# A streaming-encoder layer on one core: rows normalised before the up projection, its convolution read from PSUM, the embedding product placed in front of it

## Chip, cores and metric

The kernel runs on one core of a Trainium2 chip. The metric is the device time of one execution in microseconds (us); several executions are made and their median is given. The profile is of one execution.

## The reference, cut to what matters

The input is 2048 rows of 1024 columns in float32. One layer is computed:

```
x = x + concat(conv mixer, RWKV-7 mixer)(rms_norm(x) @ w_in) @ w_out
u = causal_dwconv(rms_norm(x) * ffn_norm_g @ ffn_w_up, conv_w) + conv_b      # width 3 in time, 5632 columns
x = x + (silu(u[:, :2816]) * u[:, 2816:]) @ ffn_w_down
e = rms_norm(p @ ple_w_proj)                                                # p has 256 columns
x = x + sigmoid(rms_norm(x) @ ple_w_gate) * e
out = rms_norm(x)
```

rms_norm divides each row of x by the root of the mean of its squares and multiplies by a gain per column. The convolution takes, for each column, the value of this time step and of the two before it.

## The kernel before

Everything lies transposed: columns of x on the 128 partitions, time along the free dimension. Time is cut into four groups (g) of G = 512 steps. A product is made in three matmuls for each 128x128 block of the weight (`mm3`, lines 187 to 193), since weight and row are each split into a high and a low part of type fp32r: hi x hi, hi x lo, lo x hi. An up product has 8 blocks, 24 matmuls of 128x512, and lands in one PSUM tile of tag "d" in the pool `psd` (3 buffers, line 940), which it shares with the down products (`ps_d`), the embedding's products (`ps_e`) and the sums of the norms (`ps_norm`).

Weights are loaded in halves of 128x1024 (`half`, lines 156 to 173), 4 buffers, each for 12 matmuls. In group 0 a half is loaded from the input, its high part is a ScalarE cast and its low part a GpSimd subtraction (line 154), and the pair is stored to DRAM; in groups 1 to 3 the pair is loaded by a DMA that GpSimd issues (line 161).

A dense group is `dense_rest` (line 387), a generator:

- output projection: 8 products over the rows of y; VectorE adds x from DRAM (line 395) to give tile x2[m]. `rows.add` (line 404) then squares it (ScalarE, line 227), adds the squares up (VectorE, line 229) and splits x2[m] times its gain into hi (ScalarE, line 214) and lo (VectorE, line 215). These rows are not yet divided by the root mean square.
- up projection: 44 products in 22 pairs (`act_pair`, line 423; gate column block i and value block 22 + i), whose result is multiplied by rstd behind the product. rstd (lines 233 to 251) is a matmul of the summed squares with a matrix of ones, then a chain of ScalarE Ln, Exp and Square, each of the first two with a table load, and three VectorE operations. The first two up products don't wait for it: `product` (lines 269 to 288) copies them to SBUF (`raw`, line 281) and issues the norm behind the second (HELD = 2).
- the evacuation of an up product (lines 409 to 420): VectorE multiplies PSUM by rstd into `zb` (line 255), a tile with two more columns in front; GpSimd copies the last two columns of the previous group there (line 256) and keeps this group's last two (line 257); ScalarE multiplies by the third tap and adds the bias (line 412); VectorE adds the two other taps by shifted reads of `zb` (line 417, twice). A pair then goes through tanh (line 429), two VectorE products (lines 430 and 433) and a split into hi and lo (lines 153 and 154).
- down projection (`down`, line 440) in six stages: after every second pair of a block of four, 8 products of 12 matmuls over the four pairs before; VectorE adds them to x2 (line 457).
- embedding: `ple_rows` (line 348) loads two tiles of p and splits them after the second pair; `ple_embed` (line 358) makes 8 products of 6 matmuls after the third pair, in four weight quads with a yield after each; ScalarE copies each to SBUF (line 370), stores it to DRAM (line 371) and squares it. Its rstd comes after the fourth pair.
- gate projection: 8 products, then the last norm and the store of the output, which is issued within the next group (line 405).

Beside it runs the RWKV mixer as a second generator, `rwkv_unit`, in 16 units of 128 time steps: some 41 steps each, small matmuls with long chains of VectorE, ScalarE and DMA between them. `drive` (line 978) lets it take one step for each yield of the dense generator (0.85 in the output and gate projections). It ends shortly before group 3's dense work.

TensorE's instructions stay in program order (`pin`, line 91). The order on the other engines, and the slots of the pools, are set at build time by a scheduler that takes, by a model of time, what is ready and first in priority; most evacuations and norms are marked as high priority. The pool of 128x512 work tiles (`buf`, line 198) has 6 buffers, that of the split rows (`slot`, line 206) 32.

## Time and profile before

| | us |
|---|---|
| median of 3 runs | 2909.51 (2909.09 to 2910.27) |
| the profiled execution | 2908.45 |
| its span in the trace | 2906.5 |
| TensorE busy | 2768.1 (95%) |
| VectorE busy | 1908.3 (66%) |
| GpSimd busy | 1117.4 (38%) |
| ScalarE busy | 959.9 (33%) |

The span runs from the first instruction to the last; the rest of the execution lies around it. PE is TensorE's matmuls, PEld its weight loads, DVE VectorE, ACT ScalarE, POOL GpSimd, SP the engine that issues most loads. The input projection fills the first 700 us; the four dense groups begin at 700.7, 1297.8, 1865.2 and 2419.2 us. A matmul's recorded duration contains its way through the array, so neighbours overlap, and a busy TensorE in the table is not one at its peak.

### The profile page before, as it was taken

What the parts mean: (1) busy time and instruction counts of PE and PEld (TensorE: products, weight loads), DVE (VectorE), ACT (ScalarE), POOL (GpSimd) and SP (SyncE); (2) the same over time, 40 slices, a digit from 0 to 9 for tenths busy, and PEclk for the clock granted to TensorE, in tenths of its full rate; (3) what the DMA queues carried; (4) which work ended last, traced back from release to release, by engine and by line L of the source; (5) the groups of instructions that cost most, each with busy time, mean ns of one, the idle gap of its engine ahead of it and who ended that gap; (6) DMA issues with size and microseconds to landing.
All of it is one profiled execution on the core that took longest, in us unless ns stands there. A gap on an engine that the chain in (4) does not pass through costs nothing.

```text
span 2906.5 us, 42153 instructions
## 1 busy us (share of the span) xinstructions
PE 2768.1 (95%) x15464; PEld 2226.7 (77%) x15464; DVE 1908.3 (66%) x3039; ACT 959.9 (33%) x1721; POOL 1117.4 (38%) x1700
## 2 busy tenths in 40 slices
PE   8999999999889999989999999999999999999997
PEld 5778888778677877767778887777788877788885
DVE  5575665648587868796766676857676765544446
ACT  5332232312553433443412223434222143411113
POOL 4533232324556565652333333333333332433221
PEclk9999999999999999989999999999999999999998
DMA  8887777767777777767666565766565668666665
GB/s 298 297 261 217 236 214 223 209 210 243 263 252 245 258 241 247 248 228 230 178 186 185 173 192 172 233 202 200 174 192 169 187 187 266 216 195 189 196 188 169
DMA packets 285802, 629.95 MB, mean 217 GB/s; under 512 B 60186, under 2 KB 113690, under 8 KB 285596
## 3 DMA queue, kind: packets, MB, share of 16 engines
q0 software_dynamic: 95040, 346.07, 39.4%
q1 hardware_dynamic: 134144, 232.83, 24.0%
q10 hardware_dynamic: 56412, 48.36, 5.2%
q8 instruction: 122, 2.00, 0.3%
q14 instruction: 84, 0.69, 0.1%
HBM read 467.77 MB, written 159.38 MB: 216 GB/s over the span
## 4 chain that ended last, share of the span: by engine, by line
PE 50%; DVE 22%; DMA 14%; issue 6%; ACT 5%; POOL 3%; ACTq 1%; SPq 0%; DVEq 0%; POOLq 0%
PE ps_mm L86 33%; PE ps_d L86 11%; DVE uf L417 3%; DVE pd L794 3%; DVE xs L798 2%; DMA lm<-ld 1%; DMA xd<-xs 1%; DMA ld<-ltt 1%; DVE zb L255 1%; DVE sq L229 1%; DMA es<-e 1%; PE o_ps L86 1%; DMA dt<-xd 1%; DVE lo L215 1%; DMA x<-in_xT 1%
## 5 line engine op out<-in xcount | busy, mean ns | idle before, releaser
L86 PE MATMUL ps_mm<-hi,whlu 128*128 128x512 f32 x2816 | 910.6, 397 | 11.3 <-POOL whlu L154 5.1
L86 PEld LDWEIGHTS ps_mm<-hi,whlu 128*128 128x128 f32 x2816 | 532.3, 189 | 131.9 <-POOL whlu L154 7.8
L86 PE MATMUL ps_mm<-hi,whlin 128*128 128x512 f32 x1664 | 542.9, 400 | 19.6 <-ACT whlin L153 7.1
L86 PE MATMUL ps_mm<-lo,whlu 128*128 128x512 f32 x1408 | 552.3, 392 | 1.5 <-DVE lo L215 1.5
L86 PE MATMUL ps_d<-hi,whld 128*128 128x512 f32 x1408 | 456.1, 396 | 16.7 <-DMA whld<-kd 7.2
L86 PEld LDWEIGHTS ps_mm<-hi,whlin 128*128 128x128 f32 x1664 | 316.7, 190 | 93.0 <-ACT whlin L153 7.1
L417 DVE SCALAR_TENSOR_TENSOR uf<-zb,vec,uf 128x512 f32<-128x512 f32 x352 | 298.6, 851 | 89.6 <-ACT uf L412 78.4
L86 PE MATMUL ps_mm<-lo,whlin 128*128 128x512 f32 x832 | 328.9, 395 | 2.8 <-DVE lo L215 2.8
L412 ACT ACTIVATE uf<-zb,vec 128x512 f32<-128x512 f32 x176 | 143.1, 815 | 562.0 <-DVE zb L255 536.8
L86 PEld LDWEIGHTS ps_d<-hi,whld 128*128 128x128 f32 x1408 | 265.6, 189 | 79.2 <-DVE x L457 8.4
L86 PEld LDWEIGHTS ps_mm<-lo,whlu 128*128 128x128 f32 x1408 | 266.8, 189 | 56.2 <-DVE lo L215 2.4
L161 POOL DMA_DIRECT2D whlu<-ku x264 | 141.7, 537 | 436.8 <-PE ps_mm L86 289.1
L255 DVE TENSOR_TENSOR zb<-ps_mm,rstd 128x512 f32<-128x512 f32 x216 | 148.5, 688 | 208.0 <-PE ps_mm L86 204.4
L86 PE MATMUL ps_d<-lo,whld 128*128 128x512 f32 x704 | 275.4, 391 | 0.0
L457 DVE TENSOR_TENSOR x<-ps_d,x 128x512 f32<-128x512 f32 x192 | 131.6, 687 | 139.5 <-PE ps_d L86 138.7
L86 PEld LDWEIGHTS ps_mm<-lo,whlin 128*128 128x128 f32 x832 | 158.4, 190 | 38.1 <-DVE lo L215 6.6
L161 POOL DMA_DIRECT2D whlin<-kin x156 | 84.1, 539 | 248.9 <-PE ps_mm L86 207.7
L86 PE MATMUL ps_mm<-hi,whlg 128*128 128x512 f32 x512 | 169.2, 406 | 3.4 <-DMA whlg<-kg 3.4
L86 PE MATMUL ps_mm<-hi,whlo 128*128 128x512 f32 x512 | 163.1, 397 | 8.5 <-DMA whlo<-ko 4.9
L154 POOL TENSOR_TENSOR lo<-th,hi 128x512 fp32r<-128x512 f32 x88 | 115.2, 1310 | 110.9 <-ACT hi L153 110.3
L154 POOL TENSOR_TENSOR whlu<-rawu,whlu 128x512 fp32r<-128x512 f32 x88 | 122.6, 1398 | 88.9 <-ACT whlu L153 79.2
L86 PEld LDWEIGHTS ps_d<-lo,whld 128*128 128x128 f32 x704 | 133.2, 189 | 26.0
(205 smaller groups left out, 4248.0 us busy)
## 6 DMA issues: line engine op xcount, KB each, us to landing
whlu<-ku POOLq DMA_DIRECT2D x264, 512.0 KB, 4.5
whlin<-kin POOLq DMA_DIRECT2D x156, 512.0 KB, 4.8
whld<-kd POOLq DMA_DIRECT2D x132, 512.0 KB, 4.0
ku<-whlu SPq DMA_DIRECT2D x88, 512.0 KB, 4.7
kin<-whlin SPq DMA_DIRECT2D x52, 512.0 KB, 5.3
whlo<-ko POOLq DMA_DIRECT2D x48, 512.0 KB, 5.5
whlg<-kg POOLq DMA_DIRECT2D x48, 512.0 KB, 3.9
rawu<-in_w_up SPq DMA_DIRECT2D x88, 256.0 KB, 4.1
```

Of the source, the lines that this page charges most:

```text
L86: return pin(nc.tensor.matmul(*args, **kw))
L154: nc.gpsimd.tensor_tensor(out=lo, in0=raw, in1=hi.bitcast(F32), op=ALU.subtract)
L161: nc.gpsimd.dma_start(out=t, in_=kept[key])
L215: nc.vector.scalar_tensor_tensor(out=lo, in0=src, scalar=gcol, in1=hi.bitcast(F32), op0=ALU.mult, op1=ALU.subtract)
L229: nc.vector.tensor_tensor(out=sq, in0=sq, in1=self.acc, op=ALU.add)
L255: nc.vector.tensor_tensor(out=zb[:, 2 : G + 2], in0=ps, in1=rstd, op=ALU.mult)
L412: nc.scalar.activation(u, zb[:, 2 : G + 2], AF.Identity, bias=v("ffn_conv_b", n), scale=v("ffn_conv_w", 88 + n),)
L417: nc.vector.scalar_tensor_tensor(out=u, in0=zb[:, d : d + G], scalar=v("ffn_conv_w", 44 * d + n), in1=u, op0=ALU.mult, op1=ALU.add,)
L457: nc.vector.tensor_tensor(out=x2[m], in0=ps, in1=x2[m], op=ALU.add)
L794: tt(out=pd[:, :, :, 0:n], in0=xs[:, :, None, 0:n].broadcast_to([P, 8, 2, n]), in1=lm[:, None, i : i + 2, 0:n].broadcast_to([P, 8, 2, n]), ...
L798: nc.vector.tensor_reduce(out=xs[:, :, i : i + 2], in_=pd[:, :, :, 0:n], op=ALU.add, axis=mybir.AxisListType.X,)
```

## The change

- The output stage only sums the squares; it no longer splits rows. After the fifth output product (m = 4) the p tiles are loaded and split.
- After the output products come the first quad of the embedding, a yield, the norm's matmul and chain, and then, for each of the 8 rows, a VectorE product x2 * gain * rstd, a ScalarE cast to hi and a subtraction to lo, on VectorE for even and GpSimd for odd rows. The three other quads of the embedding follow, and only then the up products. The embedding's own norm comes after the first pair.
- An up product is evacuated from PSUM without zb: ScalarE makes tap and bias, and copies the last two columns to u_last; VectorE adds two columns from the new tile `halo` to the first two and then adds the two other taps with the PSUM tile itself as shifted input. `halo` is made for all 44 products at once, in four operations of 128x44, in front of the rows.

```
--- before.py
+++ after.py
@@ -18,7 +18,7 @@
 G = 512
 KD = 8
 FIN = 1
-PLE_AT = 2
+PLE_ROWS = 4
 HELD = 2
 WAIT = 20
 R_BONUS = 1
@@ -142,6 +142,7 @@
     z_last = cpool.tile([P, 14], F32, tag="z_last", name="z_last")
     cx_last = cpool.tile([P, 4, 2], F32, tag="cx_last", name="cx_last")
     u_last = cpool.tile([P, 44, 2], F32, tag="u_last", name="u_last")
+    halo = cpool.tile([P, 44, 2], F32, tag="halo", name="halo")
     for t in (z_last, cx_last, u_last):
         nc.vector.memset(t, 0.0)
 
@@ -388,7 +389,7 @@
         tmp = pools["tmp"]
         gs = slice(g * G, (g + 1) * G)
         x2 = []
-        rows = Rows()
+        rows, ss = Rows(), SumSq()
 
         def evac_o(ps, _):
             t = pools["x2"].tile([P, G], F32, tag="x2", name=f"x2_{g}_{len(x2)}")
@@ -401,22 +402,55 @@
                 xs.append(staged(pools, xT[m, :, gs], "xr"))
             for _ in product(pools, weight(pools, w_out[m], f"o{m}"), yrows, evac_o):
                 yield SLOW
-            rows.add(pools, x2[m], v("ffn_norm_g", m))
+            ss.add(pools, x2[m])
             if m == FIN and pending:
                 pending.pop()()
+            if m == PLE_ROWS:
+                prows = ple_rows(pools, g)
+
+        embedding = ple_embed(pools, g, prows)
+        next(embedding)
+        yield
+        rstd = ss.rstd(pools)
+        with tc.high_priority():
+            w0, w1 = v("ffn_conv_w", 0, 44), v("ffn_conv_w", 44, 44)
+            nc.vector.tensor_tensor(out=halo[:, :, 1], in0=u_last[:, :, 1], in1=w0, op=ALU.mult)
+            nc.vector.tensor_tensor(out=halo[:, :, 0], in0=u_last[:, :, 1], in1=w1, op=ALU.mult)
+            nc.vector.tensor_tensor(out=u_last[:, :, 0], in0=u_last[:, :, 0], in1=w0, op=ALU.mult)
+            nc.vector.tensor_tensor(
+                out=halo[:, :, 0], in0=halo[:, :, 0], in1=u_last[:, :, 0], op=ALU.add
+            )
+            for k in range(KD):
+                xn = buf(pools, "xn")
+                nc.vector.scalar_tensor_tensor(
+                    out=xn, in0=x2[k], scalar=v("ffn_norm_g", k), in1=rstd,
+                    op0=ALU.mult, op1=ALU.mult,
+                )
+                hi, lo = pair(pools)
+                nc.scalar.copy(hi, xn)
+                eng = nc.gpsimd if k % 2 else nc.vector
+                eng.tensor_tensor(out=lo, in0=xn, in1=hi.bitcast(F32), op=ALU.subtract)
+                rows.hs.append((hi, lo))
+        for _ in embedding:
+            yield
+        rows.ss = None
 
         def up(n, st, key):
-            def evac(ps, rstd):
-                zb = scaled(pools, ps, rstd, u_last[:, n, :], 2)
+            def evac(ps, _):
                 u = st[key] = buf(pools, "uf")
                 nc.scalar.activation(
-                    u, zb[:, 2 : G + 2], AF.Identity,
+                    u, ps, AF.Identity,
                     bias=v("ffn_conv_b", n), scale=v("ffn_conv_w", 88 + n),
                 )
-                for d in (1, 0):
+                nc.scalar.copy(u_last[:, n, :], ps[:, G - 2 : G])
+                nc.vector.tensor_tensor(
+                    out=u[:, 0:2], in0=u[:, 0:2], in1=halo[:, n, :], op=ALU.add
+                )
+                for d in (1, 2):
                     nc.vector.scalar_tensor_tensor(
-                        out=u, in0=zb[:, d : d + G], scalar=v("ffn_conv_w", 44 * d + n),
-                        in1=u, op0=ALU.mult, op1=ALU.add,
+                        out=u[:, d:G], in0=ps[:, 0 : G - d],
+                        scalar=v("ffn_conv_w", 88 - 44 * d + n), in1=u[:, d:G],
+                        op0=ALU.mult, op1=ALU.add,
                     )
             return product(pools, weight(pools, w_up[n], f"u{n}"), rows, evac)
 
@@ -468,11 +502,7 @@
                 if i == first + 2 and prev is not None:
                     yield from down(first - NB, prev)
                 yield from act_pair(i, acts)
-                if i == PLE_AT - 1:
-                    prows = ple_rows(pools, g)
-                if i == PLE_AT:
-                    yield from ple_embed(pools, g, prows)
-                if i == PLE_AT + 1:
+                if i == 0:
                     embed[g] = embed[g].rstd(pools)
             if len(acts) <= 2:
                 yield from down(first - NB, prev)
```

## Rows read from the trace of the kernel before

**Rows 1.** Stretches: transitions of groups 2 and 3, then up/down of groups 0 to 3.
```profile
core 0: us, PE busy (x) PEld busy (x) DVE busy (x) ACT busy (x) POOL busy (x), PEclk, DMA share, GB/s
...
1911.90:1945.70 33.80, 29.85 (x242) 22.70 (x241) 16.31 (x27) 13.13 (x20) 10.36 (x20) 0.95 0.58 165
2464.60:2487.00 22.40, 22.40 (x98) 18.20 (x97) 8.45 (x13) 9.09 (x12) 5.36 (x12) 1.00 0.62 176
781.60:1229.60 448.00, 420.64 (x2515) 335.14 (x2513) 348.29 (x498) 193.72 (x363) 266.90 (x269) 0.98 0.72 247
1381.30:1804.20 422.90, 412.94 (x2537) 333.43 (x2535) 291.60 (x503) 122.47 (x234) 151.38 (x271) 0.99 0.61 181
1945.70:2366.10 420.40, 411.04 (x2537) 332.49 (x2535) 290.91 (x502) 121.36 (x231) 150.00 (x270) 1.00 0.60 180
2487.00:2840.20 353.20, 350.59 (x1541) 288.70 (x1541) 164.73 (x237) 80.72 (x120) 115.78 (x236) 1.00 0.67 200
```

**Rows 2.** TensorE's waits, 781.6 to 1229.6 (group 0): total, times, longest us.
```profile
PE ps_mm L86 <- POOL whlu L154: 5.1, 6, 1.4
PE ps_d L86 <- DVE x L457: 4.0, 3, 1.7
...
PE ps_o L86 <- DVE arb L754: 0.4, 2, 0.3
```

**Rows 3.** TensorE's waits, 1381.3 to 1804.2 (group 1).
```profile
PE ps_d L86 <- DMA whld<-kd: 3.4, 2, 2.1
PE ps_g L86 <- DVE suv L655: 2.8, 2, 2.5
```

**Rows 4.** TensorE's waits, 1945.7 to 2366.1 (group 2).
```profile
PE ps_g L86 <- DVE suv L655: 3.1, 1, 3.1
```

**Rows 5.** TensorE's waits, 2487.0 to 2840.2 (group 3).
```profile
PE ps_e L86 <- ACT e L370: 1.2, 2, 0.7
```

**Rows 6.** Up matmuls: all groups by form, with idle time before them and its releasers.
```profile
L86 PE MATMUL ps_mm<-hi,whlu 128*128 128x512 f32 x2816 | 910.6, 397 | 11.3 <-POOL whlu L154 5.1 <-ACT hi L214 4.6 <-DMA whlu<-ku 1.3
L86 PE MATMUL ps_mm<-lo,whlu 128*128 128x512 f32 x1408 | 552.3, 392 | 1.5 <-DVE lo L215 1.5
```

**Rows 7.** Groups of the page: busy us, mean ns of one, idle before.
```profile
L417 DVE SCALAR_TENSOR_TENSOR uf<-zb,vec,uf 128x512 f32<-128x512 f32 x352 | 298.6, 851 | 89.6 <-ACT uf L412 78.4
...
L412 ACT ACTIVATE uf<-zb,vec 128x512 f32<-128x512 f32 x176 | 143.1, 815 | 562.0 <-DVE zb L255 536.8
...
L154 POOL TENSOR_TENSOR lo<-th,hi 128x512 fp32r<-128x512 f32 x88 | 115.2, 1310 | 110.9 <-ACT hi L153 110.3
```

**Rows 8.** GpSimd's halo copies, groups by form, whole span.
```profile
L257 POOL COPY u_last<-zb 128x2 f32<-128x2 f32 x176 | 59.8, 340 | 62.7 <-DVE zb L255 62.3
L256 POOL COPY zb<-u_last 128x2 f32<-128x2 f32 x176 | 56.0, 318 | 41.3 <-DVE uf L417 37.7 <-DVE xs L798 2.1 <-DVE pd L794 0.7
```

**Rows 9.** Tile zb: duration ns min/median/max, first and last start us.
```profile
L417 DVE SCALAR_TENSOR_TENSOR uf<-zb,vec,uf x352: 707/751/1856, 771.7 to 2810.7; 128x512 f32<-128x512 f32 x176
L255 DVE TENSOR_TENSOR zb<-ps_mm,rstd x216: 676/691/694, 45.1 to 2807.8; 128x512 f32<-128x512 f32 x108
```

**Rows 10.** Tiny operations of ScalarE and VectorE, groups by form, whole span.
```profile
L635 ACT COPY nrd<-ksum 64x4 f32<-64x4 f32 x64 | 12.3, 192 | 20.4 <-DVE ksum L631 19.7
...
L590 DVE TENSOR_TENSOR gam<-ep,em 128x4 f32<-128x4 f32 x16 | 2.5, 157 | 0.0
```

**Rows 11.** Timeline of VectorE, transition of group 3: start us, us, instruction, idle before.
```profile
2464.81 0.69 DVE L395 TENSOR_TENSOR x<-ps_mm,xr 128x512 f32<-128x512 f32 x1 [2.68 <-PE ps_mm L86]
2466.20 0.69 DVE L229 TENSOR_TENSOR sq<-sq 128x512 f32<-128x512 f32 x1 [0.70 <-ACT sq L227]
...
2478.31 0.69 DVE L240 TENSOR_SCALAR ms<-ps_norm 128x512 f32<-128x512 f32 x1 [10.74 <-ACT rstd L239]
...
2481.64 0.69 DVE L248 SCALAR_TENSOR_TENSOR rstd<-nt,rstd 128x512 f32<-128x512 f32 x1
```

**Rows 12.** Timeline of ScalarE, the same transition.
```profile
2476.29 1.28 ACT L239 ACT_TABLE_LOAD   x1
```

## The prediction

> **What bounds the kernel now.** I read the busy shares by stage first, then the chain of waits for TensorE in each of those stages, then the durations of the operations that the diff touches, and last a timeline of one transition from output to up projection.
>
> The stages show TensorE as the bound: it is busy in 411 to 421 us of each long up/down stretch of groups 0 to 2, and VectorE, the next engine, in 291 to 348 us [rows 1]. In group 3, where no RWKV steps are left, 1541 matmuls fill 350.6 of 353.2 us, so there is nearly nothing to win there. The transition of group 3 gives the unit for everything below: 98 matmuls in 22.40 us, 0.229 us each, so 12 matmuls (the distance from one yield to the next) are 2.7 us and an up product of 24 is 5.5 us.
>
> What a lighter VectorE and GpSimd could give back is TensorE's idle time that ends on them. In group 0 that is thirteen entries from 5.1 us (GpSimd's split of the up weights) to 0.4 us, together 27.3 us [rows 2]; in group 1 the only large one that ends on an engine is 2.8 us, in group 2 3.1 us, both of the RWKV unit [rows 3, 4]; in group 3 it is 1.2 us of the embedding's own copies [rows 5]. The sum is 33 us, plus what the clock gives: group 0's stretch has a mean granted clock of 0.98, part of it at the lower of the two levels (1.2 instead of 2.4 GHz), so about 0.02 x 448 = 9 us lie there. This is the ceiling of the gain in the up stage. Rows that reach the up product late cost 4.6 + 1.5 = 6.1 us in the whole kernel today [rows 6].
>
> **The change, part by part.**
>
> *Up evacuation.* Removed per up product are VectorE's multiplication by rstd (median 691 ns) and two GpSimd copies of two columns (340 and 318 ns, 59.8 + 56.0 us over 352 instructions, with waits for VectorE in front of them that also hold GpSimd's weight splits) [rows 8, 9]. The two convolution steps now have PSUM as their first input. Today, with both inputs in SBUF, they take 707 to 1856 ns, mean 851, while the operation on a PSUM tile takes 676 to 694 [rows 7, 9]; I take 690 for the new form (bounds 690 and 851). Added are a two-column ScalarE copy (192 ns for a comparably tiny one) and a two-column VectorE add (157 ns for 128x4) [rows 10]. VectorE saves 691 + 2 x 161 - 157 = 0.86 us per product, 38 us per group, 150 us in all; ScalarE gains 34 us of work. None of it is on TensorE, so its worth is only what it takes out of the 33 us. VectorE's share in group 0 falls from 78% to 69%, and GpSimd is rid of the copies that block its splits. I take 60%: **-20 us**, with -5 us for clock that is not lost. Bounds: 0 and -42.
>
> *The row norm moves onto the path.* Today each row is split while the output products run, and rstd is applied behind the up product, whose first two results wait in SBUF for it. After the change no up matmul can start before rstd. The timeline of group 3 gives the pieces [rows 11, 12]: from the last output evacuation to the last sum of squares 2466.20 + 0.69 - 2464.81 = 2.1 us, hidden by the first embedding quad (12 matmuls, 2.7 us); then the two ones matmuls (at least 0.5); then from ScalarE's table load to the end of rstd 2481.64 + 0.69 - 2476.29 = 6.0 us. rstd stands 2.7 + 0.5 + 6.0 = 9.2 us after the last output product. Behind it come eight multiplications and four subtractions on VectorE, two-SBUF forms at some 0.75 (median), 9.0 us, and four subtractions on GpSimd at 1.31, 5.2 us [rows 7, 9].
>
> Do these two lie beside each other? The 1856 ns maximum of a two-SBUF operation, 1.1 us above its median, against 694 at most for one with a PSUM input, says that they exclude each other [rows 9]. The Trainium skill has the rule: SBUF — State Buffer, section "Who interferes with whom", says that a VectorE instruction with two SBUF inputs contends with a GpSimd instruction that reads SBUF, and that the loser blocks for the whole instruction. The trace agrees (1856 against 694); if it did not hold, the stall below would be 3.2 us per group in place of 7.1, and the sum some 16 us lower.
>
> One behind the other, the last row stands at 9.2 + 14.2 = 23.4 us, and its three matmuls end at 24.1. TensorE has 48 embedding matmuls (11.0), the ones matmuls (0.5) and the first up product (5.5), 17.0 us of work: it idles 7.1 us. Side by side the last row stands at 9.2 + 9.0 + 1.3 = 19.5 and the idle time is 3.2. If the six later VectorE additions of the embedding's squares (0.69 each) come between, it is 7.1 + 4.1 = 11.2. I take 8, nearest to the middle case. In groups 0 to 2 RWKV steps give TensorE cover (its transition in group 2 is 33.8 us with 242 matmuls, against 22.4 and 98) but load VectorE too; I let the two cancel, with 0 as the lower bound there. Group 0 splits its weights on GpSimd in the same stretch, so I add 3. **+35 us** (bounds 3 and 52).
>
> *Clock.* Group 2's transition, in which TensorE waits for a row, has a mean clock of 0.95 over 33.8 us, 0.05 x 33.8 = 1.7 us lost [rows 1]. Four idle stretches of 8 us should each cost as much: **+7**, and the present 1.7 goes.
>
> *Removed waits.* The late rows of today, **-6**; the clock above, **-2**; the embedding's wait in group 3, **-1**.
>
> *Moves with no price.* The embedding's four yields stay four, so RWKV's steps keep their count. Its p loads on SP and their splits go into the output stage. The four weight halves go ahead of the up weights in GpSimd's queue, 12 matmuls behind each as before; the eight stores of the embedding leave ScalarE's queue earlier. If this cover fails the first quad waits for a load as a down product does today, 2.1 us at the longest [rows 3], once per group: 8 us, inside the range. The four tiny halo operations run while VectorE waits for rstd. The two held raw copies vanish from ScalarE. The embedding's own norm comes after the first pair instead of the fourth; its chain was and is beside up products.
>
> Sum: 35 + 7 - 6 - 2 - 1 - 20 - 5 = **+8 us** on the profiled execution's 2908.45 us. The median of the runs, 2909.51, stands 1.06 above it: 2917.
>
> **The rivals.**
>
> *The burst is hidden and the relief is real (faster).* RWKV steps fill the transitions of groups 0 to 2 and only group 3 pays 3.2 us; two thirds of the 33 us and of the 9 us clock come back, and today's 9 us of waits and their clock go: 3 - 22 - 6 - 9 = -34, 2875. For it: VectorE is idle for 10.7 us before rstd in group 3 today [rows 11], and the embedding is 11 us of cover. Against: the rows only begin when that cover is nearly used up. Chance 0.30.
>
> *It cancels (same).* TensorE's order is fixed and VectorE is no bound, so neither term is over 6 us after the other is taken off: 2904 to 2915. Chance 0.20.
>
> *PSUM is held too long (slower).* The tile is now free after ScalarE's 815 ns, the small copy and add, and two convolution steps, 0.82 + 0.19 + 0.16 + 1.38 = 2.6 us with no queue, against 0.69 today [rows 7, 9, 10]. With three buffers, the third down product behind an up product needs it back after two of 2.7 us, so it decides once VectorE and ScalarE come more than 2.9 us late. In group 0 this end already shows in x's 4.0 us in three waits, 1.3 each [rows 2]. Six down stages in four groups at 1 us are 24 us more than my forecast, 2941. The Trainium skill's PSUM — Partial Sum Buffer, section "Summary: rules for kernel authors", asks to evacuate promptly; no row here yet shows a conv step holding a tile. Chance 0.12.
>
> **How the numbers follow.** The forecast, a small loss, has 0.38 and a range of its own of 2912 to 2940. A measurement of this kernel can tell about 0.2%, 5.8 us. Faster: 0.30 and 0.03 from the lower edge of the cancelling case, 0.33. Same: 0.17 of that case and 0.03 of the forecast's lower edge, 0.20. Slower: 0.35 and 0.12, 0.47. The range takes in the faster rival down to 2878 and the PSUM rival up to 2950; a tenth of the chance lies on either side.
>
> **What would show it.** Right, if TensorE's rows name the row operands (hi, lo) as releasers of the first up product in all four groups with some 8 us each, if the convolution steps read about 690 ns with no 1.8 us maximum, if group 0's waits for the weight splits shrink by half, and if the clock falls at the transitions. Wrong, if the first up product of group 3 starts without a wait, if group 0's long stretch loses less than 10 us, or if down products start to wait for the up evacuation.

## The result and the profile after

The changed kernel takes 2949.41 us (median of 4 runs, 2946.26 to 2954.84) against 2909.30 for the kernel before in the same comparison (2902.08 to 2910.27). The ratio is 1.0145, with a 95% interval of 1.0126 to 1.0164. It is slower by some 40 us where 8 were forecast, and lies above the forecast's own range of 2912 to 2940. The profiled execution took 2946.26 us, its span is 2944.4.

| us | before | after |
|---|---|---|
| TensorE busy | 2768.1 (95%) | 2774.3 (94%) |
| VectorE busy | 1908.3 (66%) | 1834.6 (62%) |
| GpSimd busy | 1117.4 (38%) | 1035.9 (35%) |
| ScalarE busy | 959.9 (33%) | 959.5 (33%) |
| mean granted clock | 0.984 | 0.973 |
| input projection (code unchanged) | 700.7 | 704.8 |
| four output stages | 190.8 | 204.0 |
| embedding, up and down of four groups | 1766.2 | 1787.1 |
| four gate stages | 234.0 | 232.9 |

A stage runs here from its first matmul to the first of the next. The engines that the change relieves are relieved, 74 us on VectorE and 82 on GpSimd, and TensorE, which sets the end, doesn't follow: 13 us more lie in the output stages and 21 in the embedding and up/down stages. The 4 us in the input projection lie in code that is the same in both. Over the profiles of all kernels below, that stage read 697.7 to 709.4 us; I put no cause to it. So a difference of a few us in a stage, between two single executions, says little by itself.

First the stretches of the kernel after, which answer to [rows 1]: the embedding stages of groups 0 and 3, the first four up products of group 3, the rest of up/down of groups 0 to 3, and the output stage of group 3.

```profile
core 0: us, PE busy (x) PEld busy (x) DVE busy (x) ACT busy (x) POOL busy (x), PEclk, DMA share, GB/s
752.00:784.20 32.20, 19.31 (x146) 13.72 (x144) 21.51 (x27) 22.36 (x38) 13.55 (x9) 0.73 0.68 256
2492.00:2518.30 26.30, 15.66 (x52) 11.14 (x51) 18.31 (x23) 18.27 (x28) 8.70 (x8) 0.74 0.54 160
2518.30:2540.70 22.40, 22.40 (x98) 18.20 (x97) 10.82 (x18) 9.26 (x15) 5.90 (x9) 1.00 0.66 195
812.70:1239.00 426.30, 404.39 (x2417) 324.92 (x2415) 300.39 (x487) 176.72 (x374) 227.77 (x184) 0.98 0.72 247
1420.20:1818.40 398.20, 392.52 (x2407) 318.72 (x2405) 261.31 (x488) 106.69 (x247) 120.81 (x181) 1.00 0.62 182
1989.70:2389.20 399.50, 393.92 (x2407) 319.49 (x2406) 261.24 (x487) 105.54 (x244) 120.02 (x180) 1.00 0.61 179
2540.70:2878.50 337.80, 337.80 (x1491) 279.47 (x1490) 132.51 (x221) 65.11 (x136) 92.54 (x145) 1.00 0.67 195
2441.50:2492.00 50.50, 46.96 (x195) 37.66 (x194) 21.05 (x31) 11.94 (x17) 10.99 (x18) 0.96 0.84 268
```

The embedding stage of group 3 takes 26.3 us for 52 matmuls, at a mean granted clock of 0.74; by the prediction's unit (12 matmuls in 2.7 us) they are some 12 us of work. The up products behind them take the 22.40 us that the transition took before, at a clock of 1.00. So the price of the row norm is paid in the embedding, not at the first up product. The long stretches are shorter than in [rows 1], but they hold fewer matmuls as well, since the embedding has left them, so the two can't be subtracted.

TensorE's waits over the whole span, the four that matter (total, times, longest, us):

```profile
PE ps_e L86 <- ACT e L371: 40.5, 8, 8.8
PE ps_mm L86 <- DMA whlo<-ko: 14.4, 6, 4.5
...
PE ps_d L86 <- DVE x L491: 11.7, 6, 3.7
...
PE ps_mm L86 <- POOL whlu L155: 5.7, 3, 2.5
```

Before, the first, the third and the fourth were 1.2 us [rows 5], 4.0 and 5.1 us [rows 2]. The second, and one that belongs with the third, read then:

```profile
PE ps_mm L86 <- DMA whlo<-ko: 4.9, 2, 4.5
...
PE ps_d L86 <- DVE zb L255: 2.9, 5, 1.0
```

In the row of zb a down product waits for the PSUM tile of an up product. The largest wait of the changed kernel is new: an embedding product waits for ScalarE's copy of an earlier one, twice in each group, 10.1 to 10.2 us per group. The second is the output product waiting for the load of its weights. The third is the down product waiting for a PSUM tile. The fourth was to shrink and did not.

The up matmuls by form, with the idle time before them, answer to [rows 6]:

```profile
L86 PE MATMUL ps_mm<-hi,whlu 128*128 128x512 f32 x2816 | 903.9, 395 | 6.9 <-POOL whlu L155 5.7 <-DMA whlu<-ku 1.2
L86 PE MATMUL ps_mm<-lo,whlu 128*128 128x512 f32 x1408 | 549.8, 390 | 0.0
```

No up matmul waits for a row any more, neither for its high nor for its low part.

The new evacuation, by tile (duration in ns as min/median/max, first and last start), answers to [rows 9]:

```profile
L450 DVE SCALAR_TENSOR_TENSOR uf<-ps_mm,vec,uf x352: 731/748/752, 792.3 to 2849.4; 128x511 f32<-128x511 f32 x176
L441 ACT ACTIVATE uf<-ps_mm,vec x176: 760/781/787, 790.8 to 2846.1; 128x512 f32<-128x512 f32 x176
L446 DVE TENSOR_TENSOR uf<-uf,halo x176: 117/160/1251, 791.8 to 2846.9; 128x2 f32<-128x2 f32 x176
...
L464 DVE SCALAR_TENSOR_TENSOR th<-th,uf x88: 677/692/798, 800.7 to 2847.4; 128x512 f32<-128x512 f32 x88
```

The convolution steps have lost their maximum of 1856 ns, but not their median: 748 against 751. The two-column add is 160 ns at the median and 1251 at most.

Now the embedding stage of group 3, in order of time (start us, us, instruction, idle before it and its releaser):

```profile
2501.57 0.69 DVE L249 SCALAR_TENSOR_TENSOR rstd<-nt,rstd 128x512 f32<-128x512 f32 x1
2502.30 4.41 DVE L425 SCALAR_TENSOR_TENSOR xn<-x,vec,rstd 128x512 f32<-128x512 f32 x5
2503.08 2.61 ACT L430 CAST hi<-xn 128x512 fp32r<-128x512 f32 x4 [2.27 <-DVE xn L425]
2504.45 3.38 POOL L432 TENSOR_TENSOR lo<-xn,hi 128x512 fp32r<-128x512 f32 x2 [5.07 <-ACT hi L430]
...
2507.86 0.58 ACT L371 COPY e<-ps_e 128x512 f32<-128x512 f32 x1 [0.51 <-POOL lo L432]
...
2508.50 0.80 PE L86 MATMUL ps_e<-hi,whlpj 128*128 128x512 f32 x1 [7.85 <-ACT e L371]
...
2510.83 1.76 DVE L425 SCALAR_TENSOR_TENSOR xn<-x,vec,rstd 128x512 f32<-128x512 f32 x1
...
2513.39 1.55 POOL L432 TENSOR_TENSOR lo<-xn,hi 128x512 fp32r<-128x512 f32 x1 [1.34 <-ACT hi L430]
...
2513.78 0.79 PE L86 MATMUL ps_e<-hi,whlpj 128*128 128x512 f32 x1 [2.35 <-ACT e L371]
```

Read it from the middle. TensorE stands for 7.85 us in front of an embedding product, until ScalarE's copy of an earlier one has made a PSUM tile free. That copy stands behind five casts of rows in ScalarE's queue, and what releases it is GpSimd's subtraction of a row's low part: it needs a work tile, the five rows that VectorE has just multiplied hold five of the six, and a tile comes back only when a row's low part is done. So the embedding, meant as cover for the rows, waits for the rows.

The row chain itself came as forecast. rstd is done at 2502.26, and the last row at 2513.39 + 1.55 = 2514.94, 22.9 us after the last output product (2492.0); 23.4 were worked out. The two parts differ more than the sum: rstd took 10.3 us and not 9.2, the rows behind it 12.7 and not 14.2. In groups 1 and 2 the chain has 23.5 and 22.9 us, in group 0 27.0.

Last, the output stage of group 3, the same view:

```profile
2461.22 7.53 ACTq L549 DMA_DIRECT2D out<-o  x7
...
2464.47 6.32 SPq L204 DMA_DIRECT2D p<-in_pT  x2
...
2465.03 0.53 POOL L162 DMA_DIRECT2D whlo<-ko  x1 [2.19 <-PE ps_mm L86]
...
2471.36 0.61 ACT L154 CAST hi<-p 128x512 fp32r<-128x512 f32 x1
...
2472.05 1.28 POOL L155 TENSOR_TENSOR lo<-p,hi 128x512 fp32r<-128x512 f32 x1 [6.49 <-ACT hi L154]
...
2473.29 1.63 POOL L162 DMA_DIRECT2D whlo<-ko  x3
...
2475.67 0.62 ACT L154 CAST hi<-p 128x512 fp32r<-128x512 f32 x1 [2.22 <-DMA p<-in_pT]
```

GpSimd issues the loads of output weights one by one, each behind a matmul that frees a buffer (2.7 us apart before and up to 2465.03 here). Then p's low part stands at the head of its queue and waits 6.49 us for ScalarE's cast of p. That cast has two things in front of it here: the output stores of the group before in ScalarE's own queue, and the load of p, asked for at 2464.47 and landed at 2470.93, 0.4 us before the cast. The second tile of p waits for its load alone (last line), and so do the first tiles of groups 1 and 2, whose casts start 0.02 us after the load has landed. Three loads go out at once when it ends, and TensorE waits 3.5 us for the weights.

### The profile page after: what moved, and what is told of

Its sections match the earlier page's. It is cut to its first block, busy times and chain, and to the rows that moved or that the text cites. A ratio compares the mean times of both kernels' runs of the same rounds, so it can differ in the third digit from the quotient of the medians.

```text
span 2944.4 us, 41885 instructions
## 1 busy us (share of the span) xinstructions
PE 2774.3 (94%) x15464; PEld 2230.8 (76%) x15464; DVE 1834.6 (62%) x3071; ACT 959.5 (33%) x1889; POOL 1035.9 (35%) x1364
## 4 chain that ended last, share of the span: by engine, by line
PE 56%; DVE 20%; DMA 12%; issue 4%; ACT 4%; POOL 2%; SPq 1%; ACTq 0%; DVEq 0%; POOLq 0%
PE ps_mm L86 35%; PE ps_d L86 13%; DVE pd L824 3%; DVE xs L828 2%; DVE uf L450 2%; DMA lm<-ld 2%; PE ps_e L86 1%; DMA ld<-ltt 1%; PE o_ps L86 1%; DVE xn L425 1%; DMA xd<-xs 1%; DMA dt<-xd 1%; DMA x<-in_xT 1%; DVE sq L230 1%; DMA e<-es 1%
## 5 line engine op out<-in xcount | busy, mean ns | idle before, releaser
L86 PE MATMUL ps_d<-hi,whld 128*128 128x512 f32 x1408 | 456.8, 397 | 18.6 <-DVE x L491 11.7
L441 ACT ACTIVATE uf<-ps_mm,vec 128x512 f32<-128x512 f32 x176 | 137.1, 779 | 546.0 <-PE ps_mm L86 494.4
L450 DVE SCALAR_TENSOR_TENSOR uf<-ps_mm,vec,uf 128x511 f32<-128x511 f32 x352 | 262.6, 746 | 13.9 <-ACT u_last L445 2.6
L446 DVE TENSOR_TENSOR uf<-uf,halo 128x2 f32<-128x2 f32 x176 | 46.7, 265 | 232.6 <-ACT uf L441 152.3
L162 POOL DMA_DIRECT2D whld<-kd x132 | 71.8, 544 | 233.7 <-PE ps_d L86 139.0
L86 PEld LDWEIGHTS ps_d<-lo,whld 128*128 128x128 f32 x704 | 133.7, 190 | 26.3
```

The lines of the kernel that those rows point to most:

```text
L86: return pin(nc.tensor.matmul(*args, **kw))
L162: nc.gpsimd.dma_start(out=t, in_=kept[key])
L441: nc.scalar.activation(u, ps, AF.Identity, bias=v("ffn_conv_b", n), scale=v("ffn_conv_w", 88 + n),)
L446: nc.vector.tensor_tensor(out=u[:, 0:2], in0=u[:, 0:2], in1=halo[:, n, :], op=ALU.add)
L450: nc.vector.scalar_tensor_tensor(out=u[:, d:G], in0=ps[:, 0 : G - d], scalar=v("ffn_conv_w", 88 - 44 * d + n), in1=u[:, d:G], op0=ALU.mult ...
```

## The experiments

Four questions, a few kernels each. Every ratio is to the kernel before, with its 95% interval; each kernel has a profile of its own. A difference between two of these ratios has an interval of some 0.003 either way, 8 to 9 us.

### What holds the embedding: the shared tiles, or the row chain

**Rows' tiles in another pool.** Theory A: the wait is that of the six shared work tiles. Theory B: it is the length of the row chain, and comes out somewhere in any case.

```diff
-                xn = buf(pools, "xn")
+                xn = pools["x2"].tile([P, G], F32, tag="x2", name="xn")
```

> The changed kernel with one edit: the eight normalised rows take their tiles from the two spare x2 buffers, no longer from the six work buffers that the embedding's copies also need. Theory A (the embedding's copies wait for work buffers that the rows hold, so its PSUM tiles stay full): TensorE's wait for the copies falls from 10 us per group to under 3, the time from 2949 to about 2915 to 2925. Theory B (the row chain of norm, VectorE and GpSimd is what takes the time, the buffers only decide where it shows): the wait comes back in front of the first up product, about as long, and the time stays within 8 us of 2949.

Measured: 1.0076 (1.0051 to 1.0100). TensorE's waits:

```profile
PE ps_mm L86 <- DVE lo L432: 7.3, 9, 1.6
...
PE ps_mm L86 <- POOL lo L432: 6.2, 12, 1.9
...
PE ps_mm L86 <- ACT hi L430: 3.4, 5, 1.6
...
PE ps_e L86 <- ACT e L371: 2.7, 5, 0.7
```

The wait of 40.5 us is 2.7, and 20 us of the time are back (1.0145 less 1.0076). The other part has become waits of the up products for their rows, 7.3 + 6.2 + 3.4 = 16.9 us. The first four up products of group 3 took 30.9 us where they took 22.4. A holds for the wait that the trace shows, and B for what is left when it is gone: the rows were to come back "about as long", and came back less than half as long.

**Rows behind the embedding.** The row loop is issued after the three other quads, so that the embedding has its tiles first.

```diff
+        for _ in embedding:
+            yield
+        with tc.high_priority():
             for k in range(KD):
...
-        for _ in embedding:
-            yield
```

> The changed kernel with the row loop issued behind the remaining embedding quads, so that the embedding's copies come first on ScalarE. Theory A: no wait within the embedding, a wait for rows of some 5 us per group in front of the up product, time 2925 to 2935. Theory B: the rows start as late as the embedding ends, the wait moves to the first up product and is 10 us or more per group; time 2945 to 2960.

Measured: 1.0143 (1.0116 to 1.0171), as slow as the change itself. The embedding's wait is 2.6 us, and the up products wait 19.9 us for ScalarE's high parts (four times, 5.5 at most) and 10.1 us for VectorE's low parts. Who goes first only moves the wait.

**The embedding back where it was, rows without cover.**

```diff
-        embedding = ple_embed(pools, g, prows)
-        next(embedding)
-        yield
         rstd = ss.rstd(pools)
...
-        for _ in embedding:
-            yield
...
+                if i == 2:
+                    yield from ple_embed(pools, g, prows)
```

> The changed kernel with the embedding (and the p loads) back behind the third pair, so that the rows have no cover at all but the norm's own matmuls. The row chain of the prediction (23 to 24 us from the last output product to the last row, of which the up product itself covers 5.5) then shows as some 15 to 18 us of waiting for rows per group, at low clock, against 12 us per group of waiting in the embedding now: 2955 to 2990, less about 13 for the p splits that leave the output stages, 2942 to 2977. If the embedding in front of the up products costs more than it covers, the time is under 2940.

Measured: 1.0196 (1.0177 to 1.0216).

```profile
PE ps_mm L86 <- ACT hi L425: 25.1, 4, 6.3
PE ps_mm L86 <- DVE lo L427: 18.0, 4, 4.5
PE ps_norm L86 <- DVE sq L230: 17.3, 5, 5.2
```

Without cover TensorE waits 25.1 + 18.0 = 43.1 us for the rows, 10.8 per group, and 17.3 for sums of squares, which cost 6.6 in the changed kernel. By the ratios, the embedding's place in front is worth 15 us (1.0196 less 1.0145), or 24 with the 9 that its p tiles cost in the output stage (next question): it is 44 us of work, so by this estimate about half of it serves as cover.

### What the p tiles cost in the output stage

**p's low part on VectorE.** Theory C: the output stage is longer because GpSimd stands behind p's low part while loads of weights queue behind it.

```diff
-                residual(t, hi, lo)
+                nc.scalar.copy(hi, t)
+                nc.vector.tensor_tensor(out=lo, in0=t, in1=hi.bitcast(F32), op=ALU.subtract)
```

> The changed kernel with the low part of the two p tiles made on VectorE instead of GpSimd. Theory C (the p splits, waiting for late p loads, stand in GpSimd's queue in front of the output weights' loads): TensorE's waits for those loads in the output stages of groups 1 to 3 fall from 14.3 to about 5 us, as before the change, and the time falls by 8 to 14 us to about 2937. Rival: the loads are late because the DMA engines are full there (share 0.9): no change in those waits and in the time.

Measured: 1.0113 (1.0089 to 1.0137), 9 us better than the change. The wait for the output weights and, behind it, the output stage of group 3 (columns as in the stretches above):

```profile
PE ps_mm L86 <- DMA whlo<-ko: 8.1, 5, 4.8
```

```profile
2434.50:2479.20 44.70, 44.70 (x195) 36.41 (x194) 21.97 (x33) 11.94 (x17) 8.45 (x16) 1.00 0.92 300
```

The stage has 44.7 us again (45.4 before, 50.5 after) for the same 195 matmuls, at a clock of 1.00. The rival, that the DMA engines are full there, does not fit: they are busier in the faster stage (0.92 against 0.84). The 9 us are hardly more than their interval, but the profiles of all kernels agree. The four output stages together read 203 to 211 us in the six kernels that let GpSimd split p there, 192 to 201 in the five that use VectorE, and 190 to 195 in the five that split p later in the group and have up products to cover the norm (the kernel before is one). C holds. The wait that the prediction priced at nothing was there, on GpSimd's queue, which carries the loads.

**Both repairs.** The two edits above together.

> The changed kernel with both repairs, own tiles for the normalised rows and the p splits on VectorE. If theories A and C are separate losses that add, the time is 23 + 13 us below the changed kernel, about 2913, and what is left over the kernel before is the wait of the first up product for its rows, 8 to 12 us per group. If they are one loss seen twice, it stays near 2925.

Measured: 1.0047 (1.0030 to 1.0065). The two gains, 20 and 9 us, add up whole, and the kernel is still slower than the one before. Of what is left, the trace names 6.5 + 5.4 + 2.7 us of waits for the rows at the first up products, and 12.9 us of down products waiting for VectorE's x (11.7 in the change, 4.0 before). By stages, its profile has 201 us in the four output stages (190.8 before) and only 4 us more than before in embedding, up and down.

### What the lighter evacuation is worth

**Evacuation alone,** in the kernel before.

```diff
-                zb = scaled(pools, ps, rstd, u_last[:, n, :], 2)
                 u = st[key] = buf(pools, "uf")
                 nc.scalar.activation(
-                    u, zb[:, 2 : G + 2], AF.Identity,
+                    u, ps, AF.Identity,
...
+                for d in (1, 2):
```

> The kernel before with only the evacuation changed (taps read from PSUM, halo tile). The division by the root mean square in front of the up projection is left out; the norm itself is still computed. Theory D (the gain of the change is the relief of VectorE and GpSimd, some 20 to 30 us): 2875 to 2890. Rival (what the up stretches gained came from moving the embedding and the row splits out of them): 2900 to 2912. If PSUM held longer costs something, waits of down products for the up evacuation show over 10 us and the time is over 2912.

Measured: 0.9974 (0.9958 to 0.9990), 8 us. As this kernel leaves out the division, its first two up products have no held copies and wait for no rstd either, so the 8 us are not of the evacuation alone: in the profile, 12 of the 22 us that embedding, up and down lose lie in the long stretches and 10 in the transitions. In group 0 the long stretch falls from 448.0 to 434.9 us; in groups 1 and 2 it has 419.4 and 423.4 us against 422.9 and 420.4 [rows 1]. The waits show the price:

```profile
PE ps_d L86 <- DVE x L474: 15.4, 9, 3.7
```

4.0 us before, all of it in group 0. Now groups 1 and 2 have 3.1 and 4.9 us of it too. An up product's tile is now held until the second convolution step is done, while the row names the addition that empties an earlier down product's tile, which stands in VectorE's queue among these steps. In the longest such wait of the changed kernel, 3.73 us in group 0, operations of the RWKV unit stood in front of both (877.79 to 880.63). How much is due to the held tile and how much to VectorE being late is not shown.

**The old evacuation in the changed kernel.** The other way round: rows and embedding as changed, VectorE copies PSUM to zb.

```diff
+                zb = tmp.tile([P, G + 2], F32, tag="zb", name="zb")
+                nc.vector.tensor_copy(zb[:, 2 : G + 2], ps)
+                nc.gpsimd.tensor_copy(zb[:, 0:2], u_last[:, n, :])
+                nc.gpsimd.tensor_copy(u_last[:, n, :], zb[:, G : G + 2])
...
-                for d in (1, 2):
+                for d in (1, 0):
```

> The changed kernel with the old way of evacuating an up product put back (VectorE copies PSUM to zb, GpSimd copies the two halo columns, the convolution reads zb); rows and embedding as changed. Theory (relief of the up evacuation is worth some 10 us, as measured alone before): ratio 1.017 to 1.020. Rival 1 (the relief is worth the 20 to 30 us that the up stretches lost in the changed kernel): 1.022 to 1.026, with waits for the GpSimd weight splits back. Rival 2 (holding PSUM costs more than the relief gives): 1.010 to 1.014, with the down products' waits for x back at 4 us.

Measured: 1.0186 (1.0156 to 1.0216), 12 us worse than the change. Its four long stretches:

```profile
814.90:1245.80 430.90, 406.98 (x2417) 326.15 (x2415) 338.93 (x484) 176.04 (x333) 264.02 (x267) 0.98 0.71 245
1425.10:1827.50 402.40, 395.75 (x2407) 320.77 (x2405) 283.24 (x485) 106.02 (x206) 146.66 (x264) 0.99 0.60 180
2000.40:2401.70 401.30, 395.68 (x2406) 320.95 (x2405) 282.59 (x483) 105.12 (x203) 144.57 (x263) 0.99 0.60 178
2557.70:2895.50 337.80, 337.80 (x1491) 279.49 (x1491) 152.37 (x222) 64.58 (x95) 106.05 (x226) 1.00 0.65 195
```

These have the matmuls of the stretches after, and can be subtracted: 430.9 - 426.3, 402.4 - 398.2, 401.3 - 399.5 and 337.8 - 337.8 are 4.6 + 4.2 + 1.8 + 0 = 10.6 us. VectorE was saved 1057.1 - 955.5 = 102 us for it, GpSimd 100. The same lines settle what shortened the long stretches of the changed kernel: they sum to 1644.5 us before [rows 1], to 1572.4 here and to 1561.8 after, so 72 of the 83 us went with the embedding, the rows and the RWKV matmuls that now lie beside them, and 11 with the evacuation.

**The same with both repairs.**

> As zb_after, with the rows' tiles in a pool of their own and p's low part on VectorE (with direct evacuation that pair gave 1.0047). Theory (relief about 10 us): 1.007 to 1.010. Rival 1 (relief 20 to 30 us): 1.012 to 1.015. Rival 2 (PSUM held costs more): 1.000 to 1.004.

Measured: 1.0075 (1.0050 to 1.0099) against 1.0047 with the direct evacuation, 8 us. Each of these differences is hardly larger than its interval; what supports the figure is that three pairs of kernels and the stretches give 8 to 12 us. The single profiles spread more: the embedding, up and down stages of the three pairs differ by 22, 7 and 14 us. GpSimd's waits for weight splits, the rival's sign, are 3.1 us here and 3.6 in the kernel before this one, less than the change itself has (5.7).

**The small copy first.** The two-column add often waits for ScalarE's copy to u_last (93.0 us in all). Theory F: issued ahead of the tap, that copy no longer holds the tile.

```diff
+                nc.scalar.copy(u_last[:, n, :], ps[:, G - 2 : G])
                 u = st[key] = buf(pools, "uf")
...
-                nc.scalar.copy(u_last[:, n, :], ps[:, G - 2 : G])
```

> The changed kernel with the two-column copy to u_last issued in front of ScalarE's tap instead of behind it, so that no other ScalarE work comes between the tap and VectorE's two reads of the same PSUM tile. Theory F (the tile is held too long, because the copy waits in ScalarE's queue and VectorE's steps wait for the copy; down products pay): TensorE's waits of ps_d for VectorE fall from 11.7 us to 6 or less and the time by 4 to 10 us. Rival (VectorE is simply late there, whatever the copy does): those waits and the time stay within 3 us.

> The same edit in the kernel before with the direct evacuation alone. The division by the root mean square in front of the up projection is left out. Theory F: from 2896 to 2885 to 2892, waits of ps_d for VectorE from 15.4 to under 9 us. Rival: no change.

Measured: 1.0175 (1.0156 to 1.0195) in the changed kernel, and 1.0005 (0.9990 to 1.0021) with the evacuation alone. The down products now wait for the convolution itself as well:

```profile
PE ps_d L86 <- DVE uf L450: 11.9, 6, 2.8
...
PE ps_d L86 <- DVE x L491: 7.8, 4, 2.7
```

F's remedy fails: 11.9 + 7.8 = 19.7 us of waits for PSUM where the change has 11.7 and 0.3. The rival's "within 3 us" fails as well; why the waits grow is not shown. With both repairs it gives 1.0088 (1.0063 to 1.0114) against 1.0047, a miss too.

> The changed kernel with all three repairs: own tiles for the rows, p splits on VectorE, the copy in front. If all losses found so far are separate: 2905 to 2918, what is left being the wait for rows. If theory F fails it stays at about 2920 to 2926.

### What moving the embedding costs by itself

**The move alone,** in the kernel before.

```diff
+            if m == 4:
+                prows = ple_rows(pools, g)
+
+        yield from ple_embed(pools, g, prows)
...
-                if i == PLE_AT:
-                    yield from ple_embed(pools, g, prows)
```

> The kernel before with only the embedding (and the p loads and splits) moved in front of the up products; rows and evacuation as before. Theory E (a good part of what the up stretches gained is the embedding no longer meeting RWKV's chain and the up evacuations): up stretches of groups 1 and 2 lose about 5 us of waits each, the output stages gain theory C's 10 to 14, so 2905 to 2915. Rival (the embedding's place is worth nothing there, only the p splits cost): 2913 to 2922.

Measured: 1.0067 (1.0043 to 1.0091), 19 us, where at most 12 were expected. Two waits stand out:

```profile
PE ps_y L89 <- DVE on L590: 15.7, 3, 9.9
PE ps_mm L86 <- DMA whlo<-ko: 14.5, 7, 4.3
```

The second is theory C's. The first is one of 9.9 us in group 0, where an RWKV step stands in the queue of a VectorE that works without a gap from 797.06 us to the end of the wait at 811.08, mostly on up products; the changed kernel has only 2.0 us of it. In group 3, which has no RWKV steps, the embedding took 10.9 us, all of it work.

**The move with p's low part on VectorE.**

> The kernel before with the embedding product and its p loads moved ahead of the up projection (this alone had a ratio of 1.0067), and now with p's low part subtracted on VectorE instead of GpSimd. Theory C (the move costs because GpSimd stands still behind p's low part while output weight loads queue behind it): waits for whlo fall from 14.5 us to about 8, output stages of groups 1 and 2 return to some 52 and 47 us, and the ratio to 1.001 to 1.003. Rival (the loss is the embedding's work itself beside the first up products and RWKV steps): the ratio stays at 1.005 to 1.008 while the whlo waits fall.

Measured: 1.0052 (1.0035 to 1.0069). The wait for output weights falls to 7.4 us and the output stage of group 2 from 53.6 to 46.0, but the 9.9 us stay. The output stages together fall from 203 to 192 us in the profiles, so C holds for them; the ratios differ by 4 us only, less than their interval, and the ratio is where the rival had it. Of the 15 us that are left, the trace names the 9.9 us of an RWKV step; the remainder is not shown. Whether it weighs the same in the changed kernel, where that wait isn't seen, is open.

### Another order

**Un-normalised rows for the first pairs.** If the row chain can't be covered, the first pairs can go on as before (with zb and rstd behind the product) while the normalised rows are made beside them, with direct evacuation from then on. Two such pairs, embedding behind the second:

```diff
+            if n % NFF < RAW:
+                return product(pools, weight(pools, w_up[n], f"u{n}"), rows, raw_evac)
+            return product(pools, weight(pools, w_up[n], f"u{n}"), nrows, evac)
```

> A version made to keep the relief without the burst: the kernel before, with its rows split without the norm for the first two pairs of up products, the normalised rows made beside them, the embedding behind the second pair, and the direct evacuation from the third pair on. If the row chain of some 24 us is hidden behind four up products (22 us) and the embedding (11 us), there is no wait for rows and the time is 2880 to 2898, at or under the evacuation alone. If VectorE has no room for it there, rows are late again and it is 2905 or more.

Measured: 1.0067 (1.0044 to 1.0090). A miss, 20 us slower than the kernel before. The rows' waits are gone but for 2.1 us, while the kernel splits every row twice, and the embedding waits 4.8 us for p's high part and 3.9 for its low part; which of these makes the 20 us was not tried. Three such pairs, embedding behind the third:

> The same with three pairs on the rows without the norm and the embedding at its old place behind the third pair: more cover (33 + 11 us), two products fewer per group with the direct evacuation. No wait for rows: 2882 to 2900. If it is slower than with two pairs by more than the interval, the direct evacuation is worth more than the cover.

Measured: 1.0161 (1.0129 to 1.0194). Here the second set of rows comes late (19.4 us of waits for VectorE's low parts, 7.4 at most, 11.3 for the high parts), a miss again; that it competes with the pairs' own evacuation is my reading and was not tried. So this kernel can't tell what the direct evacuation is worth against cover. No order that I tried beats the kernel before.

## Why the prediction was right in sign and wrong in size

**Right: the row norm on the path costs more than the evacuation gives.** The row chain, 23.4 us, measured 22.9 in group 3. VectorE and GpSimd exclude each other in it: VectorE's last multiplication takes 1.76 us beside a GpSimd subtraction of 1.67, where the two in front of it took 1.40 together. That is the Trainium skill's rule, SBUF — State Buffer, section "Who interferes with whom", and the trace agrees. So does the tail of the convolution steps, 1856 ns with two SBUF inputs and 752 with one in PSUM. All 56 steps over 800 ns of the kernel before began beside a GpSimd instruction already running, 53 of them beside a subtraction; of the new steps 64 began beside such a subtraction, and none is over 752.

**The burst: right in sum, wrong in place.** Forecast were 35 us of stall and 7 of clock, less 9 of waits that go: 33. The kernel with the old evacuation shows what rows and embedding together make: embedding, up and down take 1794.0 us there against 1766.2, 28 more. But the stall isn't where step two put it. The up products never wait; the embedding does, 10 us per group, because the rows' tiles and ScalarE's embedding copies are drawn from the same six buffers. The prediction counted instructions and engines for this stretch, and not buffers. The clock was undersized: of the embedding's 26.3 us in group 3, 10.2 are the wait for ScalarE and some 12 work, and the other 4 go with the granted clock: the matmuls behind the wait show 0.63 us each instead of 0.39, the lower of the two levels, up to 2517.4, where 1.7 us per group were forecast. The term's upper bound, 52, doesn't come out of its own parts, which make 4 x 11.2 + 3 = 48; the measured sum lies inside either. That the late rows' 6 us would go held.

**The first failed step: up evacuation, -20 and -5.** It is worth -8 to -12 by whole times. "I take 60%" of the 33 us that end on VectorE and GpSimd was the fault. Of the 27 us in group 0, 13 end on operations of the RWKV unit, 4.0 of them on ScalarE, so only some 14 end on weight splits, evacuation and a norm. Groups 1 and 2 gave together what their waits promised (4.2 and 1.8 us in the matched stretches, hardly clear of the spread of single executions); group 0, which held 27 of the 33 us, gave 4.6, or 13.1 with the evacuation alone. Group 3, where VectorE loses 152.4 - 132.5 = 20 us of work and its stretch none of its 337.8, shows what a lighter VectorE is worth where TensorE doesn't wait for it. VectorE's saving was too large as well, 150 us for all 176 products against 102 in the stretches that hold 160 of them: the convolution steps take 748 ns and not 690, the small add 265 on the mean and not 157. The waits for GpSimd's weight splits, 5.1 us, which were to halve, are 5.7. And part of the gain is handed back by the rival that had 0.12: down products wait 11.7 us for x, 4.0 before, in groups 1 and 2 now as well. With the waits for an up product's tile (2.9 us before; 0.3 and 0.5 now, for VectorE and for the small copy) it is 12.5 us against 6.9. The prediction had it as a case against the forecast; it is a term within it, of 5 to 6 us and not of the 24 that the case was given. That the measured time comes near this case's 2941 is luck. The Trainium skill's advice to evacuate promptly (PSUM — Partial Sum Buffer, section "Summary: rules for kernel authors") has its row here, 12.5 against 6.9 us.

**The second failed step: "moves with no price".** The p tiles were priced at 0, with 8 us as the end of the range if a first quad waited for a load. Shown is 13 us more in the output stages, of which p_on_vector gives back 9 of the whole time. The queue was named in the prediction (GpSimd's), but for the four embedding halves alone; what was missed is that p's low part stands in the same queue as the loads of output weights, and waits there for a cast that in turn waits for p's load, in group 3 for ScalarE's stores as well.

**The sum by the measured terms:** 28 for rows and embedding (33 forecast), -7 for the evacuation by the same two stretches (1794.0 to 1787.1; -25 forecast), 13 for the output stages (0 forecast), 4 for the input projection and -1 for the gate stages: 37 of the 37.9 us between the spans. These are differences of single executions; the split into 28 and -7 hangs on one profile, and by whole times that pair gives -12.

The signs named beforehand came out so: the clock does fall at the transitions (0.73 and 0.74), and the convolution steps have lost their maximum. But they don't read 690 ns, the waits for weight splits have not halved, and the releaser in each group is the embedding's copy and not a row. All three signs for "wrong" were there: the first up product of group 3 starts without a wait, the evacuation gives group 0's long stretch 4.6 us in the matched pair and not 10, and the down products wait longer for VectorE.

Left open: why the direct evacuation makes down products wait, by the held tile or by a late VectorE; the 9.9 us wait of the move alone in group 0, and how much of the changed kernel's groups 0 to 2 it stands for. More work tiles or a fourth PSUM buffer were not tried.

## What to carry to other kernels

Work that is to hide a chain hides it only if the two share no buffers and no queue: before an operation is counted as cover, look at the pool that its output is drawn from, and at who else holds its tiles then. An engine that issues loads must not get a computation that waits for another engine or for a load, since every load behind it waits as well. And 100 us taken off an engine that is not the bound gave 10: read the gain from the bound engine's waits in matched stretches, and count how long the new form holds its PSUM tile.

## What the runs showed of the hardware that was not expected

The convolution step with its first input in PSUM isn't shorter at the median: 748 ns against 751 with both in SBUF. The forecast's 690 was read from an operation of another form. In the changed kernel the median goes with the scalar:

```profile
L425 DVE SCALAR_TENSOR_TENSOR xn<-x,vec,rstd x32: 739/748/1762, 766.1 to 2510.8; 128x512 f32<-128x512 f32 x32
L545 DVE SCALAR_TENSOR_TENSOR o<-x,vec,rstd x32: 742/748/752, 1333.3 to 2939.7; 128x512 f32<-128x512 f32 x32
```

These have all inputs in SBUF, shift nothing and add to nothing, and take 748 ns like the convolution step; what the three share is a scalar that is a column of `vec`, one value per partition. The tanh product (line 464), also on two SBUF inputs, has the constant 1.0 as its scalar and takes 692. All scalar_tensor_tensor of 128x512 in both kernels fall into these two groups, medians of 747 to 752 with a column and 683 to 693 with a constant. Why those with a column take some 60 ns longer is not shown.

A two-column VectorE add on two SBUF inputs takes 117 to 1251 ns, with a median of 160 and a mean of 265: how small it is doesn't protect it from the waits of the large ones, and 176 of them cost 46.7 us. The 30 that take over 200 ns all began beside a GpSimd instruction already running.

A wait's cost goes on behind it. In group 3 the matmuls behind the 7.85 us stand are at the lower clock until 2517.4 us, 8.9 us after it ended, with a second wait of 2.35 us among them. With the rows' tiles in a pool of their own, the same embedding has a clock of 1.00 and takes 13.7 us.
